# Leading a transformer block in row pairs with one weight cast, positions loaded later, rotation angles on another engine

## The chip, the core and the metric

The kernel runs on one NeuronCore of a Trainium2 chip. Its engines are TensorE (PE, matmuls, with its weight loads shown as PEld), VectorE (DVE), ScalarE (ACT), GpSimd (POOL) and SyncE (SP, which here issues nearly all DMA transfers). The metric is the device time of one execution in microseconds (us); lower is better. Times of single instructions are given in ns or us.

## The reference

The block takes x (256 rows of 2048) and adds two things to it: a mixer and a squared-ReLU MLP, with RMS norms before each and at the end.

```python
def reference(x, positions, ...):
    u = _rmsnorm(h, norm_mix_g[l])
    h = h + _mixer(u, positions, w_in[l], ...)
    z = _rmsnorm(h, norm_mlp_g[l]) @ w_up[l]
    h = h + jnp.square(jax.nn.relu(z)) @ w_down[l]
    return _rmsnorm(h, norm_f_g)
```

The mixer multiplies u by a wide matrix `w_in` and cuts the product into the parts of two attention branches. The first 2048 columns are the retention's queries and keys (8 heads of 128 each). They are rotated by position:

```python
def _rope(t, positions):
    ang = positions.astype(jnp.float32)[..., None] * inv
    cos = jnp.cos(ang)[:, :, None, :]
    sin = jnp.sin(ang)[:, :, None, :]
    out = jnp.concatenate([t1 * cos - t2 * sin, t2 * cos + t1 * sin], axis=-1)
```

All data is float32. The positions are 256 consecutive integers starting somewhere below 4096.

## The kernel before

**Precision.** A float32 operand is split in two float32r parts: `hi`, a cast of the value on ACT, and `lo`, the value minus `hi` on DVE (`split`, L334; the same is written out in `weights`, L156 to L163). A product is then three matmuls. Where x is the moving operand, `hi` and `lo` of x lie beside each other in one tile, so that one 128x512 matmul does weight `hi` by both (`t_pass1`, L167) and one 128x256 matmul does weight `lo` by x `hi` (`t_pass2`, L171). The two halves of the PSUM result are added by `join` (L324): a copy of one half on ACT, an addition on DVE.

**Units.** The 2048 query and key columns of `w_in` are 16 units of 128 columns. Each unit contracts over 16 "rows" of 128 (KT = 16), so it is 16 first passes and 16 second passes. The results of a unit lie in one of four PSUM buffers (`mmps`). Units 0 to 2 are the lead; unit 3 follows in two halves (`t_half`, L444), then 4 and 5, then 6 to 15, whose results and those kept in `early` are rotated (`rope`, L493) into `qk`.

**The lead (L384 to L406).** The input `lead` holds, for each of the 16 rows, 256 columns of x transposed and 3 x 128 columns of weights of units 0 to 2, ahead of all of them 60 columns of small vectors (gains, inverse frequencies). It is loaded on SP in eight pieces of 1, 1, 2, 2, 2, 3, 3 and 2 rows into three tiles. For each piece, x is scaled by its gain and split per row (L339 on ACT, L340 on DVE), the weights are split per unit, three casts (L336) and three differences (L337) each, into tiles that hold eight rows of one unit, and the three units' passes follow. Tiles `hi` and `lo` have four slots each, raw weights five (`wtile`, L151).

**Positions and angles.** Positions are loaded right behind the lead's second piece, the same 256 integers to all 128 partitions (L397), cast to float on POOL (L411), and `angles(j)` (L414) makes two sets of angles: a product with an inverse frequency and twice a reduction by multiples of 2 pi, 17 POOL instructions per set, then two on DVE (L425, L426). `table(j)` takes sine and cosine on ACT; set 0 is multiplied by `rxb`, the inverse norm of each row of x, on POOL (L485, L486). `rxb` comes from the sums of squares of x, loaded in two halves (`load_x`, L450), a power on POOL (L441) and a small matmul (L469).

**Order.** Between engines the framework sets semaphores by data dependence. The order of the instructions on each engine is planned when the program is built, by modelled costs and the program's order; only instructions wrapped in `keep_in_program_order` hold their place among each other on their engine. In this part these are the loads on SP, and a few on ACT and POOL. SP therefore issues, in this order: lead pieces 0 and 1, positions, lead pieces 2 to 7, constants (`con`), two weight halves of unit 3, the first half of x, two weight halves of unit 4, the second half of x, and then weights as raw slots come free.

Before the lead, eight matmuls on a zeroed tile (`spin`, L359) run while nothing has been loaded.

Of the kernel before, what the change touches and what calls it, by code (L numbers as in the profile page):

```python
# [12 lines left out]
F32 = mybir.dt.float32  # L13
# [4 lines left out]
ALU = mybir.AluOpType  # L18

P = 128  # L20
S = 256
# [25 lines left out]
MAGIC = 12582912.0  # L47
INV_2PI = float(np.float32(1.0 / (2.0 * math.pi)))
# [5 lines left out]
V_MIX, V_RET, V_QA, V_KV, V_MLP, V_INV = 0, 16, 32, 36, 40, 56  # L54
N_VEC = 60
LEAD = S + 3 * P
LEAD_TILES = (0, 6, 11)
LEAD_CHUNKS = (0, 1, 2, 4, 6, 8, 11, 14, 16)
C_ID, C_MASK = 0, 128
N_CONST = 512  # L60

# [37 lines left out]
def block_kernel(ctx: ExitStack, tc: tile.TileContext, A):  # L99
    nc = tc.nc  # L100
    V, SC, G, PE = nc.vector, nc.scalar, nc.gpsimd, nc.tensor
# [8 lines left out]
    def big(name, dt=F32, shape=(P, KT, S)):  # L110
        return act.tile(list(shape), dt, tag="act16", name=name)
# [31 lines left out]
    def mmps(name):  # L143
        return pmm.tile([P, 512], F32, tag="mm", name=name)
# [6 lines left out]
    def wtile(kind, shape):  # L151
        uid[0] += 1
        dt, bufs = (F32, 5) if kind == "raw" else (F32R, 4)
        return wp.tile(shape, dt, tag=kind, bufs=bufs, name=f"{kind}{uid[0]}")

    def weights(src, shape):  # L156
        raw, hi, lo = (wtile(kind, shape) for kind in ("raw", "hi", "lo"))
        load = nc.sync.dma_start(raw, src)
        if uid[0] < 40:
            tc.keep_in_program_order(load)  # L160
        SC.copy(hi, raw)  # L161
        V.tensor_tensor(out=lo, in0=raw, in1=hi.bitcast(F32), op=ALU.subtract)  # L162
        return hi, lo  # L163

    HK = KT // 2

    def t_pass1(out, w, x, k0, n, start):  # L167
        for k in range(n):
            PE.matmul(out, w[0][:, k], x.both(k0 + k), start=start and k == 0, stop=False)  # L169

    def t_pass2(out, w, x, k0, n, stop):  # L171
        for k in range(n):
            PE.matmul(out[:, :S], w[1][:, k], x.hi(k0 + k), start=False, stop=stop and k == n - 1)  # L173

    def t_half(out, src, x, half):
        w = weights(src[:, half * HK : (half + 1) * HK], [P, HK, P])
        t_pass1(out, w, x, half * HK, HK, half == 0)
        t_pass2(out, w, x, half * HK, HK, half == 1)

    def t_unit(out, src, x):  # L180
        ws = [weights(src[:, half * HK : (half + 1) * HK], [P, HK, P]) for half in range(2)]
        for half, w in enumerate(ws):
            t_pass1(out, w, x, half * HK, HK, half == 0)
        for half, w in enumerate(ws):
            t_pass2(out, w, x, half * HK, HK, half == 1)
# [138 lines left out]
    def join(out, ps):  # L324
        t = sm.tile([P, S], F32, tag="join", bufs=2, name="join")
        SC.copy(t, ps[:, S:])
        V.tensor_tensor(out=out, in0=ps[:, :S], in1=t, op=ALU.add)
# [6 lines left out]
    def split(hi, lo, val, scale=None):  # L334
        if scale is None:
            SC.copy(hi, val)  # L336
            V.tensor_tensor(out=lo, in0=val, in1=hi.bitcast(F32), op=ALU.subtract)  # L337
        else:
            SC.activation(hi, val, AF.Copy, scale=scale)  # L339
            V.scalar_tensor_tensor(  # L340
                lo, in0=val, scalar=scale, in1=hi.bitcast(F32), op0=ALU.mult, op1=ALU.subtract
            )
# [19 lines left out]
    ip = ictx.enter_context(tc.tile_pool(name="ip", bufs=1))  # L362
# [7 lines left out]
    lead = [act.tile([P, 4096], F32, tag="act16", name=f"lead{i}") for i in range(3)]  # L370
    vec0 = lead[0][:, :N_VEC]
    x = Pair("x")
    posi = ip.tile([P, S], I32, name="posi")
    firsts = [mmps(f"first{j}") for j in range(3)]

    def lead_at(k):
        i = sum(k >= b for b in LEAD_TILES[1:])
        return lead[i], (N_VEC if i == 0 else 0) + (k - LEAD_TILES[i]) * LEAD

    def lead_x(k):  # L380
        t, o = lead_at(k)
        return t[:, o : o + S]

    wt = {}  # L384
    for k0, k1 in zip(LEAD_CHUNKS, LEAD_CHUNKS[1:]):
        n = k1 - k0
        hs = slice(k0 % HK, k0 % HK + n)
        if k0 % HK == 0:
            wt = [[wtile(kind, [P, HK, P]) for kind in ("hi", "lo")] for j in range(3)]
        t, o = lead_at(k0)  # L390
        d = N_VEC + k0 * LEAD
        skip = N_VEC if k0 == 0 else 0
        tc.keep_in_program_order(
            nc.sync.dma_start(t[:, o - skip : o + n * LEAD], A["lead"][:, d - skip : d + n * LEAD])
        )
        if k0 == 1:
            nc.sync.dma_start(posi, A["positions"].partition_broadcast(P))  # L397
        blk = t[:, o : o + n * LEAD].rearrange("p (k c) -> p k c", c=LEAD)
        for k in range(k0, k1):
            split(x.hi(k), x.lo(k), lead_x(k), scale=vec0[:, V_MIX + k : V_MIX + k + 1])  # L400
        for j, (hi, lo) in enumerate(wt):
            split(hi[:, hs], lo[:, hs], blk[:, :, S + j * P : S + (j + 1) * P])
        for ps, (hi, lo) in zip(firsts, wt):
            w = hi[:, hs], lo[:, hs]
            t_pass1(ps, w, x, k0, n, k0 == 0)
            t_pass2(ps, w, x, k0, n, k1 == KT)  # L406

    vec = cp.tile([P, N_VEC], F32, name="vec")
    tc.keep_in_program_order(G.tensor_copy(vec, vec0))
    posf = ip.tile([P, S], F32, name="posf")  # L410
    tc.keep_in_program_order(G.tensor_copy(posf, posi))  # L411
    angs = []

    def angles(j):  # L414
        ang = ip.tile([P, S], F32, name=f"ang{j}")
        G.tensor_scalar(ang, posf, vec[:, V_INV + j : V_INV + j + 1], None, op0=ALU.mult)
        kk = ip.tile([P, S], F32, name=f"kk{j}")
        step = ip.tile([P, S], F32, tag="step", name=f"step{j}")
        for _ in range(2):
            G.tensor_scalar(kk, ang, INV_2PI, MAGIC, op0=ALU.mult, op1=ALU.add)  # L420
            G.tensor_scalar(kk, kk, MAGIC, None, op0=ALU.subtract)
            for cc in (C1, C2, C3):
                G.tensor_scalar(step, kk, cc, None, op0=ALU.mult)
                G.tensor_tensor(out=ang, in0=ang, in1=step, op=ALU.subtract)
        V.tensor_scalar(ang, ang, PI_F, -PI_F, op0=ALU.min, op1=ALU.max)  # L425
        V.scalar_tensor_tensor(kk, in0=ang, scalar=-1.0, in1=ang, op0=ALU.mult, op1=ALU.max)  # L426
        angs.append((ang, kk))

    angles(0)

    early = ip.tile([P, 6, S], F32, name="early")
    for j in range(3):
# [10 lines left out]
    firsts.append(mmps("first3"))  # L443
    t_half(firsts[3], A["w_rqk"][3], x, 0)  # L444
    t_half(firsts[3], A["w_rqk"][3], x, 1)
    join(early[:, 3], firsts[3])
    xn = ip.tile([P, 2, D], F32, name="xn")
    ssx = ip.tile([P, 2], F32, name="ssx")

    def load_x(t):  # L450
        tc.keep_in_program_order(nc.sync.dma_start(xn[:, t], A["x"][t * P : (t + 1) * P]))
        SC.activation(xn[:, t], xn[:, t], AF.Square, accum_out=ssx[:, t : t + 1])
# [3 lines left out]
    t_unit(lates, A["w_rqk"][4], x)  # L456
    join(early[:, 4], lates)
    load_x(1)
    lates = mmps("first5")
    t_unit(lates, A["w_rqk"][5], x)  # L460
    join(early[:, 5], lates)
# [8 lines left out]
    rxb = rope_pool.tile([P, S], F32, tag="rxb", bufs=1, name="rxb")  # L470
# [4 lines left out]
    def table(j):  # L475
        ang, kk = angs[j]
        sgn = vec[:, V_INV + 2 + j : V_INV + 3 + j]
        cos, sin = (
            (ip if j == 0 else rope_pool).tile([P, S], F32, tag=f"{name}{j}", bufs=1, name=f"{name}{j}")
            for name in ("cos", "sin")  # L480
        )
        tc.keep_in_program_order(SC.activation(sin, ang, AF.Sin, scale=sgn))
        tc.keep_in_program_order(SC.activation(cos, kk, AF.Sin, scale=-1.0, bias=halfpi))
        if j == 0:
            G.tensor_tensor(out=cos, in0=cos, in1=rxb, op=ALU.mult)  # L485
            G.tensor_tensor(out=sin, in0=sin, in1=rxb, op=ALU.mult)  # L486
        tabs.append((cos, sin))

    table(0)
    angles(1)  # L490
    table(1)

    def rope(out, ps, cos, sin, step):  # L493
# [10 lines left out]
    for u in range(6, 2 * RH):  # L504
        ps = mmps(f"qk{u}")
# [138 lines left out]
    with ExitStack() as mctx:  # L644
        cc = big("cc", F32R, shape=(P, 2 * LT, 2, S))
# [37 lines left out]
        for k in range(0, KT, 2):  # L683
            w = weights(A["w_cq"][k // 2], [P, 2, 512])
# [4 lines left out]
        for k in range(0, KT, 2):  # L689
            for half in range(2):  # L690
                w = weights(A["w_ckv"][k // 2, half], [P, 2, 288])
# [387 lines left out]
    for n, i in enumerate((*range(ST, FT), *range(ST))):  # L1079
# [7 lines left out]
        for half in range(2):  # L1087
            w = weights(A["w_down"][i][:, half * 1024 : (half + 1) * 1024], [P, 1024])
# [128 lines left out]
```

## Time and profile before

| what | value |
|---|---|
| median of 3 runs | 1613.82 us (1612.8 to 1614.06) |
| the profiled execution | 1614.23 us |
| its span in the profile | 1612.4 us |
| mean granted TensorE clock | 0.997 |
| lead's first transfer issued, first cast of x begins | 0.72 us, 4.01 us |
| first matmul of the fourth unit (unit 3) | 27.65 us |
| first matmul of the fifth unit (unit 4) | 33.87 us |
| first matmul after the 16 units (`rv`) | 101.43 us |

The profile records one execution on the core. Times are counted from the span's start. A group or timeline line names the line of the kernel, the engine, the operation, what is written from what (`out<-in`, buffer numbers left out), shapes in partitions x elements, and a count. Where an engine was idle, the line says for how long and what ended it. "Granted clock" is the share of TensorE's full clock that the throttle let through. Two instructions that follow each other on DVE or ACT overlap a little, so the step from start to start is shorter than the duration of one. In the timeline, merged instructions show the time from the first start to the last end.

### The profile page before, as it was taken

The numbers are of one execution on the slowest core, as the hardware profiler recorded it, in microseconds if no ns is written. First come the engines' busy times: TensorE is split into PE (matmuls) and PEld (weight loads), VectorE is DVE, ScalarE is ACT, GpSimd is POOL, SyncE is SP. The second block draws the span as 40 slices with busy tenths as digits, with TensorE's granted clock in tenths as the row PEclk, the third lists the DMA queues.
The fourth block names the chain that finished last, engine by engine and source line by source line (L and its number), as shares of the span: only waits on it lengthen the run. The fifth ranks groups of instructions, "written<-read, shape, count | busy, mean of one in ns | idle before, by whom it ended". The sixth has DMA issues, their size and how long they took to land.

```text
span 1612.4 us, 21370 instructions
## 1 busy us (share of the span) xinstructions
PE 1597.1 (99%) x7966; PEld 1351.1 (84%) x7966; DVE 1045.3 (65%) x1406; ACT 861.6 (53%) x1287; POOL 69.1 (4%) x94
## 2 busy tenths in 40 slices
PE   8999999999999999999999999999999999999997
PEld 6888888888889889888888888888888888888886
DVE  7974477644446547764667689887978555555555
ACT  6544455544345446764445576666766544444444
POOL 7100000000000000000000000000000000000001
PEclk9999999999999999999999999999999999999999
DMA  8665555555556554334555666666676766666663
GB/s 310 204 228 195 191 163 165 174 194 193 192 170 208 193 196 143 121 130 144 190 215 196 229 226 234 212 230 220 219 279 235 243 215 218 218 219 217 219 211 112
DMA packets 94232, 325.31 MB, mean 202 GB/s; under 512 B 10672, under 2 KB 15920, under 8 KB 93104
## 3 DMA queue, kind: packets, MB, share of 16 engines
q1 hardware_dynamic: 91424, 313.46, 58.2%
q0 software_dynamic: 2560, 8.39, 1.9%
q10 hardware_dynamic: 144, 2.10, 0.4%
q8 instruction: 62, 1.02, 0.2%
q14 instruction: 42, 0.34, 0.1%
HBM read 311.33 MB, written 12.58 MB: 201 GB/s over the span
## 4 chain that ended last, share of the span: by engine, by line
PE 97%; DVE 1%; DMA 1%; ACT 0%; issue 0%; POOL 0%; SPq 0%; DVEq 0%; POOLq 0%; ACTq 0%
PE z L169 9%; PE dn L1074 7%; PE dn L1076 7%; PE dn L1075 7%; PE z L173 5%; PE zs L297 2%; PE zs L295 2%; PE zs L296 2%; PE qk L169 2%; PE mo L209 2%; PE rg L210 2%; PE rg L209 2%; PE rg L212 2%; PE mo L210 2%; PE mo L212 2%; PE gr L210 2%
## 5 line engine op out<-in xcount | busy, mean ns | idle before, releaser
L162 DVE TENSOR_TENSOR lo<-raw,hi 128x1024 fp32r<-128x1024 f32 (+1 forms) x430 | 519.4, 1210 | 411.0 <-ACT hi L161 408.2
L161 ACT CAST hi<-raw 128x1024 fp32r<-128x1024 f32 (+1 forms) x430 | 445.8, 1038 | 455.0 <-PE dn L1076 96.5
L1075 PE MATMUL dn<-lo,dh 128*128 128x512 f32 x512 | 199.3, 389 | 0.0
L1076 PE MATMUL dn<-hi,dl 128*128 128x512 f32 x512 | 199.3, 389 | 0.0
L1074 PE MATMUL dn<-hi,dh 128*128 128x512 f32 x512 | 197.7, 389 | 0.0
L169 PE MATMUL z<-hT,hi 128*128 128x512 f32 x640 | 159.7, 391 | 0.4 <-ACT hs L964 0.4
L169 PEld LDWEIGHTS z<-hT,hi 128*128 128x128 f32 x640 | 117.3, 188 | 23.4 <-ACT hs L964 0.8
L1076 PEld LDWEIGHTS dn<-hi,dl 128*128 128x128 f32 x512 | 96.1, 188 | 20.0
L1075 PEld LDWEIGHTS dn<-lo,dh 128*128 128x128 f32 x512 | 96.1, 188 | 19.9
L1074 PEld LDWEIGHTS dn<-hi,dh 128*128 128x128 f32 x512 | 96.0, 188 | 19.7
L337 DVE TENSOR_TENSOR lo<-raw,hi 128x1024 fp32r<-128x1024 f32 x80 | 94.9, 1221 | 18.5 <-ACT hi L336 18.4
L173 PEld LDWEIGHTS z<-hT,lo 128*128 128x128 f32 x640 | 87.3, 190 | 6.3
L173 PE MATMUL z<-hT,lo 128*128 128x256 f32 x640 | 89.2, 282 | 0.0
L336 ACT CAST hi<-raw 128x1024 fp32r<-128x1024 f32 x80 | 80.5, 1049 | 6.3 <-PE wo L210 5.0
L336 ACT CAST dh<-hl 128x256 fp32r<-128x256 f32 x64 | 25.9, 407 | 90.6 <-PE dn L1075 87.3
L336 ACT CAST shi<-forms 128x1024 fp32r<-128x1024 f32 x48 | 50.5, 1052 | 26.9 <-DVE forms L266 19.1
L1082 POOL DMA_DIRECT2D hl<-hid x32 | 17.7, 554 | 1019.4 <-DVE dl L337 550.8
L337 DVE TENSOR_TENSOR slo<-forms,shi 128x1024 fp32r<-128x1024 f32 x48 | 58.1, 1221 | 4.9 <-ACT shi L336 4.9
L964 ACT COPY hs<-z 128x512 f32<-128x512 f32 x40 | 23.4, 586 | 64.8 <-PE z L173 62.7
L337 DVE TENSOR_TENSOR dl<-hl,dh 128x256 fp32r<-128x256 f32 x64 | 27.1, 425 | 38.5 <-ACT dh L336 38.5
L209 PE MATMUL mo<-hi,my 128*128 128x512 f32 x128 | 51.0, 401 | 0.0
L209 PE MATMUL rg<-hi,x 128*128 128x512 f32 x128 | 50.7, 396 | 0.0
(323 smaller groups left out, 3190.1 us busy)
## 6 DMA issues: line engine op xcount, KB each, us to landing
raw<-w_down SPq DMA_DIRECT2D x128, 512.0 KB, 4.4
raw<-w_up SPq DMA_DIRECT2D x80, 512.0 KB, 4.4
raw<-w_rv SPq DMA_DIRECT2D x32, 512.0 KB, 4.7
raw<-w_rg SPq DMA_DIRECT2D x32, 512.0 KB, 3.7
raw<-w_gret SPq DMA_DIRECT2D x32, 512.0 KB, 4.0
raw<-w_ret_o SPq DMA_DIRECT2D x32, 512.0 KB, 4.3
raw<-w_gmla SPq DMA_DIRECT2D x32, 512.0 KB, 4.3
raw<-w_mla_o SPq DMA_DIRECT2D x32, 512.0 KB, 3.8
```

The lines of the kernel that those rows point to most:

```text
L161: SC.copy(hi, raw)
L162: V.tensor_tensor(out=lo, in0=raw, in1=hi.bitcast(F32), op=ALU.subtract)
L169: PE.matmul(out, w[0][:, k], x.both(k0 + k), start=start and k == 0, stop=False)
L173: PE.matmul(out[:, :S], w[1][:, k], x.hi(k0 + k), start=False, stop=stop and k == n - 1)
L209: PE.matmul(out, x.hi(k0 + k, ts), w[0][:, k], start=start and k == 0, stop=False)
L210: PE.matmul(out, x.lo(k0 + k, ts), w[0][:, k], start=False, stop=False)
L212: PE.matmul(out, x.hi(k0 + k, ts), w[1][:, k], start=False, stop=stop and k == nk - 1)
L336: SC.copy(hi, val)
L337: V.tensor_tensor(out=lo, in0=val, in1=hi.bitcast(F32), op=ALU.subtract)
L1074: mm(PE.matmul(out, dh[:, ts], hi[:, ws], start=i == 0, stop=False))
L1075: mm(PE.matmul(out, dh[:, ts], lo[:, ws], start=False, stop=False))
L1076: mm(PE.matmul(out, dl[:, ts], hi[:, ws], start=False, stop=end))
```

## The change

The lead goes in pieces of 1, 1 and seven times 2 rows; row 0's piece is loaded by two transfers (vectors and x, then its weights). Each piece's weights for all three units are split by one cast and one difference into one tile of `n` rows by 384 columns. Positions are loaded behind the weights of unit 3, and cast on DVE. The angles' reduction is done on DVE, where product and subtraction are one instruction; `angles(0)` comes after unit 3's `join`, `angles(1)` after the second load of x. The two products of set 0's tables with `rxb` are on DVE.

```diff
-LEAD_TILES = (0, 6, 11)
-LEAD_CHUNKS = (0, 1, 2, 4, 6, 8, 11, 14, 16)
+LEAD_TILES = (0, 6, 12)
+LEAD_CHUNKS = (0, 1, 2, 4, 6, 8, 10, 12, 14, 16)
...
-    wt = {}
     for k0, k1 in zip(LEAD_CHUNKS, LEAD_CHUNKS[1:]):
         n = k1 - k0
-        hs = slice(k0 % HK, k0 % HK + n)
-        if k0 % HK == 0:
-            wt = [[wtile(kind, [P, HK, P]) for kind in ("hi", "lo")] for j in range(3)]
         t, o = lead_at(k0)
         d = N_VEC + k0 * LEAD
         skip = N_VEC if k0 == 0 else 0
-        tc.keep_in_program_order(
-            nc.sync.dma_start(t[:, o - skip : o + n * LEAD], A["lead"][:, d - skip : d + n * LEAD])
-        )
-        if k0 == 1:
-            nc.sync.dma_start(posi, A["positions"].partition_broadcast(P))
+        cuts = (-skip, S, LEAD) if k0 == 0 else (0, n * LEAD)
+        for c0, c1 in zip(cuts, cuts[1:]):
+            tc.keep_in_program_order(
+                nc.sync.dma_start(t[:, o + c0 : o + c1], A["lead"][:, d + c0 : d + c1])
+            )
         blk = t[:, o : o + n * LEAD].rearrange("p (k c) -> p k c", c=LEAD)
         for k in range(k0, k1):
             split(x.hi(k), x.lo(k), lead_x(k), scale=vec0[:, V_MIX + k : V_MIX + k + 1])
-        for j, (hi, lo) in enumerate(wt):
-            split(hi[:, hs], lo[:, hs], blk[:, :, S + j * P : S + (j + 1) * P])
-        for ps, (hi, lo) in zip(firsts, wt):
-            w = hi[:, hs], lo[:, hs]
+        hi, lo = (wtile(kind, [P, n, 3 * P]) for kind in ("hi", "lo"))
+        split(hi, lo, blk[:, :, S:])
+        for j, ps in enumerate(firsts):
+            w = hi[:, :, j * P : (j + 1) * P], lo[:, :, j * P : (j + 1) * P]
             t_pass1(ps, w, x, k0, n, k0 == 0)
             t_pass2(ps, w, x, k0, n, k1 == KT)
...
-    tc.keep_in_program_order(G.tensor_copy(posf, posi))
...
     def angles(j):
         ang = ip.tile([P, S], F32, name=f"ang{j}")
-        G.tensor_scalar(ang, posf, vec[:, V_INV + j : V_INV + j + 1], None, op0=ALU.mult)
+        V.tensor_scalar(ang, posf, vec[:, V_INV + j : V_INV + j + 1], None, op0=ALU.mult)
         kk = ip.tile([P, S], F32, name=f"kk{j}")
-        step = ip.tile([P, S], F32, tag="step", name=f"step{j}")
         for _ in range(2):
-            G.tensor_scalar(kk, ang, INV_2PI, MAGIC, op0=ALU.mult, op1=ALU.add)
-            G.tensor_scalar(kk, kk, MAGIC, None, op0=ALU.subtract)
+            V.tensor_scalar(kk, ang, INV_2PI, MAGIC, op0=ALU.mult, op1=ALU.add)
+            V.tensor_scalar(kk, kk, MAGIC, None, op0=ALU.subtract)
             for cc in (C1, C2, C3):
-                G.tensor_scalar(step, kk, cc, None, op0=ALU.mult)
-                G.tensor_tensor(out=ang, in0=ang, in1=step, op=ALU.subtract)
+                V.scalar_tensor_tensor(ang, in0=kk, scalar=-cc, in1=ang, op0=ALU.mult, op1=ALU.add)
...
-    angles(0)
...
     t_half(firsts[3], A["w_rqk"][3], x, 1)
+    tc.keep_in_program_order(nc.sync.dma_start(posi, A["positions"].partition_broadcast(P)))
+    V.tensor_copy(posf, posi)
     join(early[:, 3], firsts[3])
+    angles(0)
...
     load_x(1)
+    angles(1)
...
         if j == 0:
-            G.tensor_tensor(out=cos, in0=cos, in1=rxb, op=ALU.mult)
-            G.tensor_tensor(out=sin, in0=sin, in1=rxb, op=ALU.mult)
+            V.tensor_tensor(out=cos, in0=cos, in1=rxb, op=ALU.mult)
+            V.tensor_tensor(out=sin, in0=sin, in1=rxb, op=ALU.mult)
...
     table(0)
-    angles(1)
     table(1)
```

## The prediction

> **What bounds the kernel now.** I read the page first: TensorE (PE) is busy for 1597.1 of 1612.4 us.
>
> ```profile
> PE 1597.1 (99%) x7966; PEld 1351.1 (84%) x7966; DVE 1045.3 (65%) x1406; ACT 861.6 (53%) x1287; POOL 69.1 (4%) x94
> ```
>
> So a change can gain only where PE waits or is clocked down. The waits of PE put 5.1 us on the first 34 us (3.4 for the lead's casts, 1.2 for the warm-up's tile, 0.3 for later weights, 0.2 for the lead's differences) and only 1.0 us on all the rest. The edits lie in the first 110 us. Next I took the start of the timeline, PE and ScalarE (ACT); the columns are start, length, engine, line, operation, and in brackets the idle time before and what ended it.
>
> ```profile
> 7.03 0.51 PE L173 MATMUL first<-x,lo 128*128 128x256 f32 x3
> 9.03 0.91 ACT L339 ACTIVATE x<-lead 128x256 fp32r<-128x256 f32 x2 [2.92 <-DMA lead<-lead]
> 10.28 1.67 PE L169 MATMUL first<-x,hi 128*128 128x512 f32 x4 [2.75 <-ACT hi L336]
> 27.77 2.01 PE L169 MATMUL first<-x,hi 128*128 128x512 f32 x8
> 33.87 3.96 PE L169 MATMUL first<-x,hi 128*128 128x512 f32 x16 [0.35 <-ACT hi L161]
> ```
>
> PE has done rows 0 and 1 at 7.54, idles 2.75 us until rows 2 and 3 have landed (9.0) and are cast, ends the lead at 27.65 (the eight at 27.77 belong to the fourth unit), and from 33.87 on the chain of waits is PE alone. Whatever moves 33.87 moves the end. The table of windows shows what happens meanwhile (PE, PEld, DVE, ACT, POOL busy, then granted clock, DMA share, GB/s):
>
> ```profile
> 3.00:4.00 1.00, 1.00 (x4) 0.31 (x3) 0.00 (x0) 0.00 (x0) 0.00 (x0) 1.00 0.99 376
> 4.00:5.00 1.00, 0.58 (x2) 0.00 (x0) 0.44 (x2) 0.99 (x4) 0.23 (x1) 1.00 0.66 150
> 5.00:6.00 1.00, 0.81 (x4) 0.71 (x5) 1.00 (x6) 1.00 (x5) 0.00 (x0) 1.00 0.39 99
> 6.00:7.00 1.00, 1.00 (x7) 0.89 (x6) 0.65 (x4) 0.11 (x1) 0.00 (x0) 1.00 0.74 264
> 7.00:8.00 1.00, 0.53 (x4) 0.30 (x2) 0.00 (x0) 0.00 (x0) 0.46 (x2) 1.00 1.02 421
> 11.00:12.00 1.00, 1.00 (x5) 0.81 (x4) 1.00 (x4) 1.00 (x4) 1.00 (x2) 0.54 1.10 461
> 12.00:13.00 1.00, 1.00 (x4) 0.84 (x4) 1.00 (x3) 1.00 (x4) 0.92 (x2) 0.50 0.95 399
> 14.00:15.00 1.00, 1.00 (x5) 0.82 (x4) 1.00 (x3) 0.75 (x3) 0.91 (x2) 0.75 0.94 397
> 16.00:17.00 1.00, 1.00 (x8) 0.87 (x7) 1.00 (x2) 0.31 (x2) 0.91 (x2) 1.00 0.97 394
> ```
>
> Three things: the transfers sink from 376 to 99 GB/s at 4 to 6 us and come back; after PE's gap the granted clock is about 0.5 from 11.0 to 14.5; VectorE (DVE) is full from 10 to 30. The DMA view of 4.25 to 5.5 us tells whose dip it is.
>
> ```profile
> DMA packets 89, 0.11 MB, mean 84 GB/s; under 512 B 12, under 2 KB 80, under 8 KB 89
> q1 hardware_dynamic: 89, 0.11, 47.4%
> ```
>
> 80 of 89 packets are under 2 KB. The lead's pieces are larger; those of positions are 128 of 1 KB, on the same queue ahead of rows 2 and 3. I take the dip for theirs.
>
> **Positions behind the lead.** By 4.25 us 0.70 MB have moved (24 GB/s for 2 us, then 0.65 MB): rows 0 and 1 (350 + 320 KB = 0.69 MB). Without positions the 640 KB of rows 2 and 3 follow at once: 0.655 MB at 418 GB/s (window 7 to 9) is 1.57 us, to 5.8. From last byte to landing the first transfer took some 0.7 us, rows 2 and 3 themselves 1.2 (bytes through at 7.8, landed 9.0); I take 0.7, since the longer tail holds the positions' stragglers: landed at 6.5 (bounds 6.5 to 8.7, the latter if positions cost only their 0.3 us of bytes). The same edit adds the split of row 0 (one more issue, 0.43 us on SP); four issues stand up to and with rows 2 and 3 in both, so that is free.
>
> DMA: Bandwidth & Descriptors, section Specifications, of the Trainium skill says that transfers of 512 B and more run at line rate; by it positions would cost 0.3 us and the kernel would come out as in rival 1. The row above (84 GB/s with 80 small packets) speaks against it.
>
> **One cast for three units.** The two activations take 0.81 us until the cast can begin (9.03 to 9.84). A 128x256 cast takes 0.40, a 128x1024 1.05; so a 128x768 some 0.83, against 0.40 until PE's first weights now. PE begins at 6.5 + 0.81 + 0.83 = 8.15, 2.1 us sooner. Its second pass needs the difference on DVE (128x768: between 0.42 for 256 and 1.22 for 1024, some 0.95), at 9.1, and two first passes cover 0.9: 0.2 lost (bounds 0 and 0.5).
>
> Then the rate. PE: first pass 3.65/16 = 0.228, second 1.91/16 = 0.119 (chain of waits), so two rows of three units cost 6 x 0.347 = 2.08 us. DMA brings two rows in 1.57. DVE, by steps from start to start where POOL is idle: 0.40 per scaled difference (two of x), 1.135 for 1024 and 0.335 for 256, hence 0.87 for 768: 1.67 per pair. ACT: 2 x 0.405 + 0.73 = 1.54. PE is the slowest, so 14 rows take 14.6 us. Before, DVE needed 17.8 us for them (9.57 to 27.37), with three differences each and POOL beside it: in the 27 to 46 stretch, with POOL at work, L162 shows 1408 ns, later 1221. Four weight slots now turn per pair, in place of three of four held for eight rows.
>
> **The clock.** Before, half clock for 3.5 us cost 1.75 us of PE work. The new gap is 7.4 to 8.15, under 1 us; the gap of 0.61 us before 5.19 left the clock at 1.00, the one of 2.75 halved it. 0.75 is nearer to the first: I take full clock.
>
> Sum: lead's end at 8.15 + 0.2 + 14.6 = 22.95 against 27.65, 4.7 us; 0.3 off for waits I can't place: **4.4 us**. It is made of 2.1 (restart), 1.75 (clock) and 1.05 (waits for DVE, since 10.28 + 14.6 + 1.75 = 26.6) less 0.5.
>
> **Angles on DVE.** Each set is 5 TENSOR_SCALAR and 6 SCALAR_TENSOR_TENSOR on 128x256, beside the two ops that were on DVE:
>
> ```profile
> L425 DVE TENSOR_SCALAR ang<-ang 128x256 f32<-128x256 f32 x2 | 0.6, 278 | 0.0
> L426 DVE SCALAR_TENSOR_TENSOR kk<-ang 128x256 f32<-128x256 f32 x1 | 0.4, 406 | 0.0
> L162 DVE TENSOR_TENSOR lo<-raw,hi 128x1024 fp32r<-128x1024 f32 x8 | 11.1, 1408 | 2.9 <-ACT hi L161 2.9
> ```
>
> 5 x 0.278 + 6 x 0.406 = 3.83, twice 7.7; the cast of positions 0.3 to 0.4; two products of tables 0.84: 8.9 us. Against it: DVE ends the lead near 20.5 in place of 27.4, eight L162 lose 0.19 each (1.5), and of 5 us idle between 28 and 50 part is filled. What hides it: the differences are early. The one of unit 8 ends at 55.8, PE wants it at 60.55; later ones lead by 6. If that cover of about 5 us went, each further us would be a us of PE. I cost it at 0. POOL drops both sets, and so the power for rx (40.09, behind an angle step, while the sum of squares stood at 37.1) comes sooner.
>
> **What is late next.** At 22.95 + 5.56 = 28.5 the fifth unit wants its weights. Up to them SP's queue holds the lead (5.27 MB), constants (0.26), two weight halves and their own two (2.10) and the first half of x (1.05): 8.68 MB, so 4.25 + (8.68 - 0.70)/0.418 = 23.3, plus positions' dip (2 us, now paid here) and 0.7: 26.0, both casts 2.0: 28.0. Covered by 0.5, and only the first half is wanted then.
>
> The profiled execution took 1614.23 us (span 1612.4); 1614.23 - 4.4 = 1609.8. The median of the runs lies 0.41 lower, so **1609.4 us**.
>
> **Rivals.** (1) The dip is not positions'. Rows 2 and 3 land at 8.7, PE starts at 10.35, half clock again: 10.35 + 0.2 + 14.6 + 1.75 = 26.9, a gain of 0.75: 1613.1. For it: rows 2 and 3, issued at 2.10, move nothing before positions do, so their own start can't be told from positions' end. Chance 0.12. (2) The clock halves all the same, since the rows bracket its limit only by 0.61 and 2.75 us. Price 1.75: 1611.2, chance 0.11. The Trainium skill, TensorE: Matmul & The Clock Gate, Part 1, has the clock fall after an idle window of some 3.4 us; this trace's 2.75 us sufficed, so the limit lies lower here than stated. (3) Given back: the join of ACT waited 2.43 us for DVE, and ACT's squares (1.92) stood ahead of the fifth unit's casts; with angles between, 2 to 4 us are lost again: 1612.5, chance 0.15. (4) **Slower**: DVE works in the order planned, and only transfers are pinned there. If the cast of positions is planned ahead of lead differences, DVE stands until positions land: lead, constants and two halves are 6.58 MB, so 4.25 + (6.58 - 0.70)/0.418 = 18.3, plus their own 2.8: 21.1. With one set of angles and the cast (4.2) 25.3, then 1.67 per pair still to do and 0.9 on PE: 26.2 + 1.67 n. One pair gives no change, from three on the lead ends at 31.2, +3.5: 1617.3. Against it: both follow the lead in the program. Chance 0.11.
>
> **How the numbers follow.** The forecast has 0.51, its own range 1608.0 to 1610.6 (bounds of the landing's tail and of the 0.2). A measurement here can tell about 0.2%, 3.2 us: faster is below 1610.6, slower above 1617.0. Faster: 0.51; slower: most of rival 4, 0.10; the rest, 0.39, within. The range begins at 1607.2, where PE never waits in the lead (48 x 0.347 = 16.7 from 4.7 on ends at 21.4, a gain of 6.25) nor at 33.87 (0.35), and reaches over rivals 1 to 3 to 1614.2.
>
> **What would show it.** Right: no dip at 4 to 6 us and one near 18 to 21; ACT's first pair of rows at 6.5; PE's gap under 1 us; granted clock 1.00 throughout; fourth unit from 23, fifth from 28.5. Wrong: PE waiting for L337 or for the cast of positions, the clock at 0.5 after 8 us, or PE idle between 28 and 60, where none was.

## The result

| | before | after |
|---|---|---|
| median (lowest to highest), 11 runs each | 1614.06 us (1612.8 to 1614.99) | 1610.07 us (1609.15 to 1612.57) |
| profiled execution, its span | 1614.23, 1612.4 us | 1610.07, 1608.3 us |
| first matmul of rows 2 and 3 | 10.28 | 9.77 |
| first matmul of the fourth unit (start in the timeline; in before the lead ends at 27.65) | 27.77 | 24.56 |
| fifth unit, sixth unit | 33.87, 39.58 | 30.14, 35.71 |
| first `rv`, last `wo` | 101.3, 908.7 | 97.4, 904.8 |

The ratio is 0.9977, with a 95% interval of 0.9969 to 0.9985: faster, since the interval lies below 1, by little more than the 0.2% that the prediction took as the least that can be told. The forecast was 1609.4. The profiled execution is 4.2 us shorter; 3.9 of it is there when the sixth unit starts, and it is carried unchanged to the last `wo`, 869 us later. PE is busy 2.7 us less (some 1.75 of it is the half clock that is gone) and POOL half as long.

```profile
PE 1594.4 (99%) x7966; PEld 1350.1 (84%) x7966; DVE 1044.0 (65%) x1416; ACT 859.6 (53%) x1272; POOL 36.4 (2%) x57
```

The start of the timeline of after, the lines that answer to those of before:

```profile
7.04 0.95 PE L169 MATMUL first<-x,hi 128*128 128x512 f32 x3 [0.80 <-DVE x L340]
7.83 0.52 PE L173 MATMUL first<-x,lo 128*128 128x256 f32 x3
8.09 0.91 ACT L339 ACTIVATE x<-lead 128x256 fp32r<-128x256 f32 x2 [1.31 <-DMA lead<-lead]
9.77 1.64 PE L169 MATMUL first<-x,hi 128*128 128x512 f32 x6 [1.42 <-ACT hi L336]
24.56 2.00 PE L169 MATMUL first<-x,hi 128*128 128x512 f32 x8
30.14 3.82 PE L169 MATMUL first<-x,hi 128*128 128x512 f32 x16
```

Rows 2 and 3 landed at 8.09 (forecast 6.5), so PE still waited twice, 0.80 and 1.42 us in place of one gap of 2.75. The line at 30.14 has no bracket: the wait of 0.35 that stood ahead of the fifth unit is gone. The windows of after (PE, PEld, DVE, ACT, POOL, granted clock, DMA share, GB/s):

```profile
2.00:3.00 1.00, 1.00 (x4) 0.43 (x3) 0.00 (x0) 0.22 (x2) 0.00 (x0) 1.00 1.00 248
3.00:4.00 1.00, 1.00 (x4) 0.32 (x3) 0.34 (x1) 0.51 (x1) 0.23 (x1) 1.00 0.85 227
5.00:6.00 1.00, 1.00 (x6) 0.87 (x6) 0.46 (x1) 0.13 (x1) 0.00 (x0) 1.00 0.92 369
11.00:12.00 1.00, 1.00 (x9) 0.94 (x8) 1.00 (x3) 1.00 (x3) 0.00 (x0) 1.00 1.00 415
12.00:13.00 1.00, 1.00 (x6) 0.83 (x6) 1.00 (x3) 1.00 (x3) 0.00 (x0) 1.00 1.01 420
20.00:21.00 1.00, 1.00 (x8) 0.91 (x7) 1.00 (x2) 0.81 (x2) 0.00 (x0) 1.00 0.88 251
```

Four things. The dip at 4 to 6 us is gone (369 GB/s at 5 to 6 us, where there were 99), and one stands at 20 to 21, where positions travel while PE is full. The granted clock is 1.00 at 11 to 13, where it was about 0.5. POOL's columns are empty from 5 us on. And a new low stands at the very start, 248 and 227 GB/s. The DMA view of 2 to 3 us shows what moves there:

```profile
DMA packets 195, 0.25 MB, mean 248 GB/s; under 512 B 16, under 2 KB 195, under 8 KB 195
q1 hardware_dynamic: 195, 0.25, 99.6%
```

All 195 packets are under 2 KB and the queue's share is 99.6%: it is full and yet moves 248 GB/s. They are row 0's two transfers, per partition 1264 B (60 columns of vectors and 256 of x) and 1536 B (384 of weights); whole, the row is one piece of 2800 B. Whether their size makes the low is asked in the first experiment.

### The profile page after: what moved, and what is told of

Read it like the earlier page. It is cut to its first block, busy times and chain, and to the rows that moved or that the text cites. A ratio compares the mean times of both kernels' runs of the same rounds, so it can differ in the third digit from the quotient of the medians.

```text
span 1608.3 us, 21340 instructions
## 1 busy us (share of the span) xinstructions
PE 1594.4 (99%) x7966; PEld 1350.1 (84%) x7966; DVE 1044.0 (65%) x1416; ACT 859.6 (53%) x1272; POOL 36.4 (2%) x57
## 4 chain that ended last, share of the span: by engine, by line
PE 97%; DVE 1%; DMA 1%; issue 0%; ACT 0%; POOL 0%; SPq 0%; DVEq 0%; POOLq 0%
PE z L169 9%; PE dn L1068 7%; PE dn L1070 7%; PE dn L1069 7%; PE z L173 5%; PE qk L169 2%; PE zs L297 2%; PE zs L295 2%; PE zs L296 2%; PE mo L209 2%; PE rg L210 2%; PE rg L209 2%; PE rg L212 2%; PE mo L212 2%; PE mo L210 2%; PE gm L210 2%
## 5 line engine op out<-in xcount | busy, mean ns | idle before, releaser
L337 DVE TENSOR_TENSOR lo<-raw,hi 128x1024 fp32r<-128x1024 f32 x80 | 94.8, 1221 | 18.2 <-ACT hi L336 18.1
L337 DVE TENSOR_TENSOR slo<-forms,shi 128x1024 fp32r<-128x1024 f32 x48 | 58.1, 1221 | 4.9 <-ACT shi L336 4.9
L209 PE MATMUL wo<-hi,mg 128*128 128x512 f32 x128 | 50.3, 393 | 0.0
```

Of the source, the lines that this page charges most:

```text
L209: PE.matmul(out, x.hi(k0 + k, ts), w[0][:, k], start=start and k == 0, stop=False)
```

## The experiments

Each kernel was timed in turns with the kernel before on the same chip; medians of before in the four groups were 1614.14 (first four), 1614.18 (next four), 1613.99 and 1613.69 (two each). "Lands" is the start of ScalarE's first activation of rows 2 and 3, and "fourth" and "fifth" the first matmul of that unit, in the profiled execution. That execution is one run and need not be typical: for six of the twelve kernels it was the slowest run, for one cast alone the second fastest. (With positions early the fourth unit is interleaved with the lead; 26.3 is worked out from 14 passes that begin at 24.89, of which the first six are the lead's, at 0.228 us each.)

| kernel | median (range), runs | ratio, 95% | lands | fourth | fifth |
|---|---|---|---|---|---|
| row 0 whole | 1609.41 (1608.58 to 1611.12), 8 | 0.9972, 0.9962 to 0.9982 | 6.63 | 24.36 | 29.95 |
| positions early | 1612.93 (1611.14 to 1614.06), 11 | 0.9992, 0.9983 to 1.0001 | 9.12 | 26.3 | 32.55 |
| positions late alone | 1610.36 (1609.24 to 1612.19), 11 | 0.9977, 0.9968 to 0.9985 | 7.18 | 24.64 | 30.22 |
| dummies in before | 1612.66 (1612.2 to 1613.18), 11 | 0.9987, 0.9978 to 0.9996 | 9.32 | 28.07 | 34.18 |
| dummies in after | 1608.86 (1608.24 to 1610.7), 6 | 0.9967, 0.9955 to 0.9979 | 7.84 | 24.88 | 30.46 |
| angles on POOL | 1609.79 (1609.26 to 1610.53), 7 | 0.9972, 0.9962 to 0.9983 | 7.63 | 24.14 | 29.73 |
| one cast alone | 1612.35 (1610.69 to 1614.05), 11 | 0.9983, 0.9974 to 0.9992 | 8.82 | 25.71 | 31.50 |
| angles with six rounds | 1612.27 (1610.7 to 1617.49), 12 | 0.9989, 0.998 to 0.9997 | 9.29 | 27.31 | 32.89 |
| row 0 whole, warm-up 10 | 1609.64 (1607.84 to 1611.57), 7 | 0.9969, 0.9958 to 0.9979 | 6.89 | 23.36 | 28.95 |
| and dummies | 1608.24 (1607.75 to 1608.77), 5 | 0.9962, 0.9948 to 0.9976 | 7.65 | 24.66 | 30.25 |
| and the order held, no dummies | 1608.83 (1608.51 to 1611.27), 7 | 0.9972, 0.996 to 0.9983 | 7.25 | 24.26 | 29.84 |
| row 0 whole, warm-up 14 | 1607.55 (1607.42 to 1608.03), 5 | 0.9959, 0.9947 to 0.9972 | 7.49 | 23.95 | 29.54 |

**Row 0 whole** (the kernel after, with row 0 in one transfer).

```diff
-        cuts = (-skip, S, LEAD) if k0 == 0 else (0, n * LEAD)
+        cuts = (-skip, n * LEAD)
```

> The changed kernel with row 0 loaded by one transfer again. Theory (small pieces slow the start): in the changed kernel the pieces of 1264 and 1536 bytes held the queue, so that row 1 landed at 5.87 us and rows 2 and 3 at 8.09; whole, row 1 lands near 5.0, rows 2 and 3 near 7.4, PE's long gap falls under 1 us, the fourth unit begins near 23.8 instead of 24.56, and the time is 0.5 to 0.8 us below the changed kernel: about 1609.4. Rival (the split helps): x of row 0 is there 0.9 us sooner with it, so whole costs up to 0.5 us: 1610.5.

Its windows:

```profile
2.00:3.00 1.00, 1.00 (x4) 0.43 (x3) 0.00 (x0) 0.22 (x2) 0.00 (x0) 1.00 0.79 215
3.00:4.00 1.00, 1.00 (x4) 0.33 (x3) 0.00 (x0) 0.00 (x0) 0.00 (x0) 1.00 0.95 321
4.00:5.00 1.00, 0.78 (x2) 0.00 (x0) 0.19 (x1) 0.73 (x2) 0.23 (x1) 1.00 1.01 405
5.00:6.00 1.00, 0.56 (x1) 0.50 (x2) 1.00 (x3) 0.99 (x3) 0.00 (x0) 1.00 1.04 420
```

The transfers are at 405 and 420 GB/s from 4 us on, where after had 287 and 369, and rows 2 and 3 land at 6.63. So the late landing of after goes with the split. That the size of the pieces makes it is not shown: from 2 to 4 us, where the small pieces travel, the whole row moves 215 and 321 GB/s against 248 and 227, about 0.06 MB more, and the lead of another 0.17 MB comes at 4 to 6 us, behind them. Together that is 0.23 MB, some 0.55 us at 420 GB/s, of the 1.46 us between the landings; the rest lies between the last bytes and the landing. The split also moves the issue of rows 2 and 3 from 1.6 to 2.1 us, and the runs do not part the two. Over all profiled executions with positions behind the lead, a whole row 0 landed rows 2 and 3 at 6.63, 6.89, 7.18, 7.25, 7.49 and 7.65, a split one at 7.63, 7.84, 8.09 and 9.29: about 1 us apart in the mean, with a spread as large within each list. The prediction's 6.5 is the early end of the first list. The medians of the two kernels (1609.41 and 1610.07) have intervals that overlap. The timeline of PE shows why 1.5 us in the landing brought only 0.2 at the fourth unit:

```profile
5.44 1.62 PE L169 MATMUL first<-x,hi 128*128 128x512 f32 x3 [0.66 <-DVE x L340]
7.50 1.48 PE L169 MATMUL first<-x,hi 128*128 128x512 f32 x3
9.42 1.80 PE L169 MATMUL first<-x,hi 128*128 128x512 f32 x6
```

Three first passes take 1.62 and 1.48 us here, and 0.95 in after: PE runs rows 0 and 1 at half rate and has no gap before rows 2 and 3, since the rows it is still at end late by as much. The granted clock column shows 1.00 there too; the rate is told by the matmuls.

**Positions early** (the kernel after, with positions back behind row 1).

```diff
         blk = t[:, o : o + n * LEAD].rearrange("p (k c) -> p k c", c=LEAD)
+        if k0 == 1:
+            tc.keep_in_program_order(nc.sync.dma_start(posi, A["positions"].partition_broadcast(P)))
...
-    tc.keep_in_program_order(nc.sync.dma_start(posi, A["positions"].partition_broadcast(P)))
```

> The changed kernel with positions loaded behind row 1 again, everything else as changed. Theory (positions make the dip): transfers fall to about 100 GB/s near 5 us, rows 2 and 3 land 1 to 2 us later (9.1 to 10), PE's gap grows to 2.5 to 3.4 us, the clock is halved for about 3.4 us, and the fourth unit begins near 10.8 + 14.6 + 1.75 = 27.2: time 1612.5 to 1613. Rival (DVE carries the gain): 24.6 to 25.5, time 1610 to 1611.

```profile
5.00:6.00 1.00, 1.00 (x3) 0.81 (x3) 0.25 (x1) 0.00 (x0) 0.00 (x0) 1.00 0.62 92
11.00:14.00 3.00, 3.00 (x9) 2.42 (x10) 3.00 (x8) 3.00 (x7) 0.00 (x0) 0.53 1.02 425
```

The dip is back (92 GB/s), rows 2 and 3 land at 9.12, the clock is at 0.53 from 11 to 14, and the median gives back 2.9 of the 4.0 us (against before, its interval still includes 1). The dip belongs to positions, which settles the prediction's first rival. The Trainium skill, DMA: Bandwidth & Descriptors, section Specifications, has transfers from 512 B on at line rate; this window, 92 GB/s with pieces of 1 KB, speaks against it, though these pieces are also one source row sent to 128 partitions, and the runs do not part the two.

**Positions late alone** (the kernel before, only the load of positions and what hangs on it moved; angles stay on POOL, three casts stay).

```diff
-        if k0 == 1:
-            nc.sync.dma_start(posi, A["positions"].partition_broadcast(P))
...
-    tc.keep_in_program_order(G.tensor_copy(posf, posi))
...
-    angles(0)
...
+    tc.keep_in_program_order(nc.sync.dma_start(posi, A["positions"].partition_broadcast(P)))
+    tc.keep_in_program_order(G.tensor_copy(posf, posi))
     join(early[:, 3], firsts[3])
+    angles(0)
```

> The kernel before with only positions moved behind unit 3's weights; casts per unit and angles on POOL stay. Theory (three needs: rows early, clock full, DVE light): rows 2 and 3 land near 7.3, the clock stays full, but DVE still needs some 17 us for 14 rows, so that the fourth unit begins near 25.7: gain 1.5 to 2.5 us, 1611.5 to 1612.5. Rival (positions alone carry it): fourth unit by 24.5, gain of 3.5 us or more, 1610.5 or less.

My theory fell here: 1610.36, as fast as the whole change. The merged cast is not needed here, since VectorE needs much less time once POOL is idle in the lead. The groups of VectorE from 8 to 28 us, first of before, then of this kernel:

```profile
L340 DVE SCALAR_TENSOR_TENSOR x<-lead,lead,x 128x256 fp32r<-128x256 f32 x10 | 6.3, 675 | 0.0
L337 DVE TENSOR_TENSOR lo<-lead,hi 128x256 fp32r<-128x256 f32 x12 | 6.2, 570 | 0.0
L337 DVE TENSOR_TENSOR lo<-lead,hi 128x384 fp32r<-128x384 f32 x6 | 4.1, 735 | 0.0
```

```profile
L337 DVE TENSOR_TENSOR lo<-lead,hi 128x256 fp32r<-128x256 f32 x12 | 4.4, 419 | 0.0
L340 DVE SCALAR_TENSOR_TENSOR x<-lead,lead,x 128x256 fp32r<-128x256 f32 x10 | 4.3, 482 | 0.3 <-ACT x L339 0.3
L337 DVE TENSOR_TENSOR lo<-lead,hi 128x384 fp32r<-128x384 f32 x6 | 3.2, 558 | 0.5 <-PE first L173 0.4
```

The same instructions take 675, 570 and 735 ns with POOL at work and 482, 419 and 558 ns without. POOL's cast of positions now starts at 21.7, and its angle steps after it. Fourteen rows took VectorE 17.8 us before and 13.4 here, and PE needs 14.6. So this one edit does three things: the early landing, the full clock, and an uncontended VectorE.

**Dummies in before** and **dummies in after**: matmuls on the zeroed tile behind rows 0 and 1 (1 and 10 in before, 3 and 6 in after), whose result is read by nothing; the matmuls of rows 0 to 3 are held in the program's order on PE.

```diff
             t_pass2(ps, w, x, k0, n, k1 == KT)
+        for _ in range({0: 1, 1: 10}.get(k0, 0)):
+            tc.keep_in_program_order(PE.matmul(spin, cold[:, :P], cold, start=True, stop=True))
```

> The kernel before with 1 and 10 matmuls on the zeroed tile put behind rows 0 and 1 on PE, whose results nothing reads, so that PE does not idle. Theory (in the kernel before DVE would bound the lead without the clock): granted clock 1.00 throughout, but DVE ends its last difference at 27.4 as before, so the fourth unit begins at 27.3 to 27.7 and the time stays within 0.5 us of 1614.1. Rival (the clock is a term that adds by itself): fourth unit near 25.9, time near 1612.3.

> The changed kernel with 3 and 6 matmuls on the zeroed tile behind rows 0 and 1 on PE, whose results nothing reads. Theory (what is left of the clock's fall makes the changed kernel's upper runs, 1612.0 to 1612.6 at a mean clock of 0.997): those runs go, all lie within 1609.2 to 1610.8, median 1609.5 to 1610.1. Rival (those runs have another cause): the spread stays, or the added matmuls hold rows 2 and 3 back and the median rises by 0.3 to 0.6.

In before, the granted clock stays at 1.00 and the lead does not end sooner. The timeline of this kernel shows why:

```profile
25.85 1.83 DVE L341 TENSOR_TENSOR lo<-lead,hi 128x256 fp32r<-128x256 f32 x3
28.07 2.00 PE L173 MATMUL first<-x,hi 128*128 128x512 f32 x8
34.18 2.12 PE L173 MATMUL first<-x,hi 128*128 128x512 f32 x8 [0.37 <-ACT hi L161]
```

VectorE's last differences (the lines moved by four) end at 27.68, in before at 27.37, and rows 2 and 3 landed later by as much (9.32, 9.03). The units begin at 28.07 and 34.18. The dummies also held rows 2 and 3 on PE to 11.72, and PE still waited 0.6 us for VectorE later in the lead: with POOL beside it VectorE set the lead's end, and the clock alone was worth nothing. So the prediction's 1.75 us for the clock could be had only together with a faster VectorE. The median fell by 1.5 us all the same, and the dummies in after took 1.2 off without a shorter lead (fourth 24.88). The first is near the rival's time without its mechanism (fourth unit at 28.07, not 25.9), and the second lies below its theory's range. This gain is not in the lead; it is followed up below.

**Angles on POOL** (the kernel after with the cast of positions, the angles and the two table products as in before, on POOL).

```diff
-    V.tensor_copy(posf, posi)
+    tc.keep_in_program_order(G.tensor_copy(posf, posi))
...
-            V.tensor_tensor(out=cos, in0=cos, in1=rxb, op=ALU.mult)
+            G.tensor_tensor(out=cos, in0=cos, in1=rxb, op=ALU.mult)
```

> The changed kernel with the cast of positions, the angles and the table products on POOL again. Theory (the lead and the place of positions carry the gain; angles cost PE nothing on either engine): PE's rows from the fourth unit to 100 us as in the changed kernel, no wait, time 1609.6 to 1610.4. Rival (POOL slows DVE's two-input instructions by a sixth and that reaches PE, or the tables come too late there): 1611 to 1612.

1609.79, the same as after within the intervals: once positions come late, the engine of the angles does not matter to the time.

**One cast alone** (the kernel before with the lead of after: pieces of two rows, one cast and one difference; row 0 whole, positions early, angles on POOL).

```diff
-        for j, (hi, lo) in enumerate(wt):
-            split(hi[:, hs], lo[:, hs], blk[:, :, S + j * P : S + (j + 1) * P])
+        hi, lo = (wtile(kind, [P, n, 3 * P]) for kind in ("hi", "lo"))
+        split(hi, lo, blk[:, :, S:])
```

> The kernel before with the lead in pairs and one cast and difference for three units, row 0 by one transfer; positions behind row 1 and angles on POOL as before. Theory (positions carry the gain, the cast alone little): the dip near 5 us stays, rows 2 and 3 land near 9, the clock is halved in most runs, PE then needs 10.5 + 14.6 + 1.75 = 26.9 against 27.65: time 1613.0 to 1613.8. Rival (the lighter DVE carries the gain): 1611.5 or less.

1612.35, a gain of 1.8, a little more than my theory's and below the rival's. The profiled execution, 1610.82, shows a full granted clock; the slowest of the eleven took 3.2 us more. The dip stays (118 GB/s at 5 to 6 us), and POOL still weighs on VectorE:

```profile
L337 DVE TENSOR_TENSOR lo<-lead,hi 128x768 fp32r<-128x768 f32 x7 | 9.0, 1292 | 0.1
```

That is 1292 ns against 956 in after. The gains of the two parts alone (1.8 here, 3.8 for positions) sum to more than the whole change brings: this fits that both take away the same wait for VectorE.

**Angles with six rounds** (the kernel after, six rounds of reduction in place of two; the four more subtract multiples of zero).

```diff
-        for _ in range(2):
+        for _ in range(6):
```

> The changed kernel with six rounds of the angles' reduction in place of two; the added rounds subtract zero multiples. It puts 4 x 2 x (2 x 0.2 + 3 x 0.35) = 11.6 us more on DVE between 26 and 60 us. Theory of the prediction (a cover of about 5 us, then 1 us of PE for each): 1615 to 1617. Rival (the differences are planned by their due times and the rotations give way): the ropes slip by 11 us, PE waits for nothing, 1609.6 to 1610.6.

VectorE is busy 10.1 us longer (1054.1 against 1044.0; 11.6 were expected), and the median is 2.2 higher. The waits of PE:

```profile
PE first L169 <- ACT hi L336: 2.9, 1, 2.9
PE qk L169 <- DVE val L327: 2.5, 1, 2.5
PE z L169 <- ACT hs L958: 1.8, 1, 1.8
```

The second line is the angles': a `join` on VectorE is late and PE has no PSUM buffer until 80.5 us. So by an estimate 7.6 of the 10.1 us were covered, and neither theory's size was right; the half clock that followed this wait (granted 0.50 from 80 to 83 us) cost PE more on top. It is not the weights' differences that slip, as the prediction had it, but the rotations: the sine table's product stands at 71.7 us here and at 46.0 in after. (The first line is the profiled execution's own bad landing, 9.29; it took 1617.49 and is the slowest of the twelve.)

**Warm-up of 10, then with dummies, with the order held, and of 14.** In these, row 0 is whole; the more matmuls of the warm-up are read by nothing.

```diff
-WARM = 8
+WARM = 10
```

> The changed kernel with row 0 in one transfer again and ten warm-up matmuls in place of eight (their result is read by nothing). Theory (what the lead of the changed kernel still loses is the small pieces of row 0, and rows 0 and 1 at half rate where the clock has not come up by their start): rows 2 and 3 landed by 6.8, no wait of PE over 0.3 us between the warm-up and 24 us, the fourth unit from 23.6 to 24.2, fifth from 29.2 to 29.9; 1608.8 to 1609.4. Rival (the two more warm-up matmuls change nothing, since the clock comes up at a time of its own): as with row 0 whole and eight warm-up matmuls, fourth unit from 24.3, 1609.4 to 1609.8.

> As the kernel with row 0 whole and ten warm-up matmuls, with one dummy matmul behind row 0 and three behind row 1 (read by nothing; rows 0 to 3 held in the program's order on PE). Theory (the lead is what counts, and it has no gap left to fill): the same as without the dummies within 0.3 us of the median, 1608.8 to 1609.6. Rival (the dummies steady the clock over the whole run, as the narrow spread of the two kernels with dummies suggests): 0.4 us or more below the kernel without them, 1608.0 to 1608.8, all runs within 1 us.

> The changed kernel with row 0 whole, ten warm-up matmuls, and the matmuls of rows 0 to 3 held in the program's order on PE as in the kernels with dummies, but with no dummies behind the rows. The kernels with dummies showed no wait of PE for hs near 935 us in the MLP and ran within 1 us of each other, though their lead was no shorter. Theory (the dummies themselves do it): as ten warm-up matmuls alone, 1609.0 to 1609.9, spread over 2 us, the wait for hs 1 us or more in the profile. Rival (the order held on PE does it): 1607.6 to 1608.6, spread of 1 us, no wait for hs.

> The changed kernel with row 0 whole and fourteen warm-up matmuls, as many added matmuls as the kernel with ten and four dummies, but all ahead of row 0 and with the order of rows 0 to 3 free (their result is read by nothing). Theory (the number of PE instructions ahead of the MLP does it): no wait for hs near 935 us, runs within 1 us, 1607.8 to 1608.8. Rival (dummies between the rows, or the order held, do it): row 0 begins near 6.2 us, rows 2 and 3 without a wait of PE, the lead as with ten, 1609.0 to 1610.0 with a spread of 2 us or more.

With ten, PE goes from the warm-up into row 0 without a wait and runs it at full rate; the fourth unit starts at 23.36, the earliest of all kernels. Yet the median, 1609.64, is no better. With dummies the lead is 1.3 us longer, and the median 1.4 us shorter. Where the difference lies is seen near 930 us, in the MLP. The waits of PE with a warm-up of 10, and with one of 14, beside the 1.2 us that each has before its warm-up:

```profile
PE z L169 <- ACT hs L958: 1.9, 1, 1.9
PE first L169 <- ACT hi L336: 0.8, 1, 0.8
```

```profile
PE first L169 <- ACT hi L336: 0.4, 1, 0.4
```

And ScalarE in the MLP, first with 10, then with 14:

```profile
932.67 0.71 ACT L336 CAST dh<-hl 128x256 fp32r<-128x256 f32 x2 [4.76 <-DMA hl<-hid]
933.29 0.58 ACT L958 COPY hs<-z 128x512 f32<-128x512 f32 x1
```

```profile
930.90 0.71 ACT L336 CAST dh<-hl 128x256 fp32r<-128x256 f32 x2 [2.39 <-DMA hl<-hid]
931.52 0.58 ACT L958 COPY hs<-z 128x512 f32<-128x512 f32 x1
```

The first load of `hl`, issued at 927.94 and 927.74 on POOL's queue, landed after 4.7 and 3.2 us. ScalarE stands before it in order, the copy of `z` behind it is late, and PE waits for its PSUM buffer. From its first to its last matmul into `z` this stage, which the change does not touch, took 343.6 to 343.8 us in the five kernels with dummies, with the order held or with a warm-up of 14, and 344.1 to 346.7 in the others (before 345.3, after 345.1). The load of `hl` is not all of it. After itself had it landed after 3.1 us and shows no such wait; its stage is longer by another wait, near 978 us, that the five do not have:

```profile
978.43 0.50 PE L297 MATMUL zs<-slo,hc 128*128 128x512 f32 x1 [0.87 <-DVE slo L337]
```

Of the expectations on record, the held order did not do it (its runs spread over 2.8 us, beside 3.7 without, although its one profile shows no wait), and the number of matmuls ahead of the lead's end goes with it: six or more added gave the narrow spreads (1.0 us over eleven runs, 1.0 and 0.6 over five each, and five of six within 0.7 with dummies in after), two added did not. But angles on POOL, with none added, spread over only 1.3 us in seven runs, so this is a pattern and no cause. Why more matmuls at the start let a load at 928 us land sooner, or keep it from landing late, I can't say; it stays open.

The kernel with row 0 whole and a warm-up of 14 has the lowest median: 1607.55, every run of it below every run of after, ratio 0.9959 (0.9947 to 0.9972), an interval that overlaps that of the dummies with a warm-up of 10. Its fourth unit starts 0.6 us ahead of after's, its MLP is 1.5 us shorter.

## Why the prediction was right, step by step

- **The total**: forecast 4.4 us, measured 4.0 in the medians and 4.2 between the profiled executions. The terms differ more than the sum. At the fourth unit the gain was 3.21, where 4.7 was forecast for the lead's end; 0.66 that the forecast had left out came in behind it, and I had taken off 0.3 for nothing in particular. That the total came so close is in part luck.
- **The signs**: no dip at 4 to 6 us, one at 20, and the full clock came as said. Rows 2 and 3 at 6.5, a gap under 1 us, the fourth unit from 23 and the fifth from 28.5 did not (8.09, 1.42, 24.56, 30.14).
- **The restart**, forecast 2.1, measured 0.51 (10.28 to 9.77). The step that was mis-sized is the landing at 6.5: 8.09, while the casts behind it took what was forecast. In it, "free" for the split of row 0 was wrong: with the row whole rows 2 and 3 land at 7.2 in the mean of six executions, split at 8.2 in the mean of four, so some 1.0 of the 1.6 is the split's, by a way that stays open. The rest is that 6.5 was the early end: one execution of the six, at 6.63, comes near it.
- **The clock**, 1.75: right, granted clock 1.00 throughout; but it was worth that only with the lighter VectorE, as the dummies in before show. The gaps here were 0.80 and 1.42, not 0.75; 1.42 is closer to the 2.75 that halved it than I assumed.
- **Waits for VectorE**, forecast 1.05: from the restart to the fourth unit after takes 14.79 us and before 17.49, 2.70 less; without the clock's 1.75 that is 0.95. This is a remainder: PE's list of waits in before has only 0.2 for VectorE in the lead. The step of VectorE per pair was 1.66 (forecast 1.67), the 128x768 cast 0.82 (0.83), its difference 0.95 (0.95), PE 2.1 per pair (2.08). The 0.2 for the second pass was about 0.1.
- **What is late next**: "covered by 0.5". The fifth unit's casts ended at 29.36 and PE wanted them at 30.14, so it held, and the 0.35 at 33.87 that I kept for the range's end came in: with what followed it, 0.66. Together 0.51 + 1.75 + 0.95 + 0.66 = 3.87, the gain at the sixth unit.
- **Angles at nothing**: right. 9.3 us of instructions by their mean durations (8.9 forecast) and no wait, and the same time on POOL. The cover was larger than my 5: about 7.6.
- **The cause**, right in part: I gave the merged cast the rate of VectorE. Positions alone give the whole gain, because they take POOL's angle steps out of the lead with them, and these slowed VectorE. The prediction had the row for it (1408 against 1221 ns) and put POOL in one clause; it did not ask what the other edits were worth with POOL gone.
- **Rival 1** fell: the dip went with positions and came back with them. Its price was about right: with the dip back, 1612.93 against 1613.1. **Rival 2** did not happen at a gap of 1.42. **Rival 3**: nothing was given back. **Rival 4**: the cast of positions stood at 21.92, behind the last difference of the lead (19.71), so its mechanism was not met. That it would cost what I priced was not tried.

## What to carry to other kernels

Do not price a small transfer by its bytes alone: a broadcast of 128 KB, 0.3 us of bytes, held back what stood behind it for 2 us, and splitting a row in two brought the next rows about 1 us later. When an engine looks full, ask first who else is at work beside it: with POOL's work out of the stretch, VectorE kept up with its 32 instructions for 14 rows as well as with 21. And do one part of a change alone before you explain the whole by all its parts.

## What the runs showed of the hardware

- POOL at work beside VectorE lengthened its instructions in the lead by 30 to 40% (482 to 675, 419 to 570, 558 to 735, 956 to 1292 ns).
- Gaps of PE and the clock after them: 2.46 us (at 80.5, with six rounds of angles), 2.75 (before) and 2.94 (in the lead with six rounds) were followed by about half clock, and so were two of 1.19 and 1.10 with positions early; two of 0.80 and 1.42 in after, and one of 1.45 with angles on POOL, were not. So no single length separates the cases. The Trainium skill, TensorE: Matmul & The Clock Gate, Part 1, says that the clock falls after an idle window of some 3.4 us and that the window runs freely, so that its phase varies from run to run. A phase that varies would fit what is seen here, but no run here shows it by itself; the length does not fit, as 2.46 us was enough.
- After the same warm-up of eight matmuls rows 0 and 1 ran at full rate in some executions (three first passes in 0.96 us in after) and at half in others (1.62 with row 0 whole), both at a granted clock of 1.00.
- A 256 KB load on POOL's queue took 3.0 to 4.8 us to land at the same place of the program, and PE waited up to 1.9 us for what stood behind it.
